# Layer 0 of a decoder trunk: the blocked part of the input projection narrowed to DeltaNet's columns

## The chip, the cores and the metric

The kernel runs on one core of one Trainium2 chip. The metric is the device time of one execution in microseconds; the figure quoted for a kernel is the median of its runs. The profile is a separate, single execution taken by the hardware profiler, and its times are read as shares and durations of that execution.

The engines are named as the profile names them: PE multiplies matrices (PEld is its loading of the stationary operand), DVE works on vectors, ACT evaluates functions and scaled copies, POOL only clears a few tiles here, and SP issues every DMA of this kernel. Each engine takes its instructions in the order in which the planner put them.

## The reference

Two layers, a sequence of 256 tokens, width 2048. In each layer a token mixer and a SwiGLU feed-forward part (FFN) follow one another, each behind an RMS norm that is shifted and scaled by a vector computed from the conditioning vector `c`:

```python
mod = c_act @ w_mod[l] + b_mod[l]                       # [2048] @ [2048, 12288]
shift1, scale1, gate1, shift2, scale2, gate2 = split(mod, 6)
h = rms_norm(x, norm1_gain[l]) * (1 + scale1) + shift1
x = x + gate1 * mixer(h)                                # w_in: 2048 -> 4888, w_out: 2048 -> 2048
h = rms_norm(x, norm2_gain[l]) * (1 + scale2) + shift2
x = x + gate2 * ffn(h)                                  # 2048 -> 2 x 5632 -> 2048
```

The mixer cuts the 4888 columns of `h @ w_in` among three parts. Gated linear attention (GLA) takes 1552 (q and k 512, v 512, gate 512, low rank 16). Sliding-window attention takes 1280 (queries 1024, keys and values 256). Gated DeltaNet takes 2056 (q 512, k 512, v 512, gate with two small vectors 520). Their outputs, 512, 1024 and 512 wide, go side by side through `w_out`. All is float32, and all of `w_mod` (201 MB for both layers), `w_in`, `w_out` and the FFN's weights are read once from HBM.

## The kernel before

**Tiles.** The 256 tokens are two blocks of 128. Activations are the stationary operand, [128 channels, 128 tokens], and weights move past them 512 columns at a time. A step of a product is one chunk of 128 rows of K and up to 1024 columns; it is called a job here (`stream`, L291 to L373). `load` (L311) issues the job's DMA into a [128, 1024] tile and `products` (L340) issues its matmuls for both blocks of tokens. After each job `tick` is called with the job's width over 1024.

**Two ways to multiply.** A split job needs ACT to round the weight (`wh`, L328) and DVE to form the exact rest (`wl`, L329); three fast products then replace one float32 product. A whole job takes the float32 weights as they are, with no work on ACT and DVE, and costs PE four passes in place of three. `WHOLE_IN`, `WHOLE_A` and `WHOLE_OUT` (L43 to L46) say which jobs are whole: in layer 0 all jobs of the blocks below, three chunks of the first GLA product and all of `w_out`; in layer 1 none of these. The weight tiles come from tags `raw`, `wh` and `wl`, three buffers each; whole jobs use the three tags in turn (L316).

**The modulation.** It is a vector times a matrix, done on DVE: `mod_segment` (L199) returns steps; each loads 128 rows of `w_mod` and adds them, times one number a partition, into an accumulator (L218, L221). `finish` (L226) later sums the accumulator over partitions, by four transposes on PE and a reduction on DVE for a shift or a scale (L246 to L254), by two matmuls for a gate (L236). The first shift and first scale of layer 0 are "early": for each block of K, one segment of 512 columns for the shift and one of 512 for the scale, their steps in turn, one DMA of 256 KB and one DVE instruction of 512 columns each; their tiles come from DeltaNet's pool. All later segments have steps of 1024 columns, 512 KB, in two buffers `mraw` and two accumulators `acc`. 96 such steps are due before layer 0's FFN: 32 for gate1, 64 for shift2 and scale2.

**Pacing.** Steps of the modulation stand in one queue, `mods`. `tick` (L271) takes `rate` steps off it for each 1024 columns of other products, and `need` (L282) takes as many as are missing when a value is needed. A step whose kind is in `closed` is not taken by `tick` until it is opened; gate1, shift2 and scale2 of layer 0 are opened as the last block of K begins (L1051). The program order that results is a priority, not the order of execution: a planner goes through the instructions before the run, puts each on its engine when it believes the operands and a free buffer to be there, and prefers what stands earlier in the program. Buffers of one tag are given out in program order.

**Layer 0 before its FFN.** K is cut into four blocks of four chunks (`K_BLOCKS`, L37), each run as soon as its shift and scale are known (loop L1048). For each block: the norm of its channels (`norm`, L436), then the products of four groups of columns (L1026): `qk` (1024), `z` (520), `v` with the keys and values of the sliding window (768), and, at the end of the block, `bq`, the queries of the sliding window (1024). After each block the sums in PSUM are added to tiles in SBUF (`land`, L966 to L975). In the last block `swa_keys` and `gdn` (L538) stand ahead of `bq`. `gdn` is a long chain of small steps: convolution (transposes at L548), decay, the inverse of a triangular matrix by doubling (L683 to L702), two blocks of state. Then comes `swa` (L881), twelve units one behind the other in one PSUM bank `ga` (scores at L897, output at L924), and the products of GLA: A1 (1024 columns, L1080) and A2 (528, L1082), from the last chunk of K to the first. `gla` (L749) uses the bank `ga` as well. `w_out` follows in two sweeps (L1112): 24 jobs over the K of the window and DeltaNet, at two steps of the modulation a job, then 8 jobs over GLA's K, at none. The second norm and the FFN come after them.

**Layer 1** runs the same code with one block of K of all sixteen chunks and all jobs split: `qk`, `z`, `v`, then `gdn`, `bq`, `swa`, A1, A2.

## Time and profile before

| | |
|---|---|
| median of 3 runs | 2591.97 us (2586.66 to 2603.76) |
| profiled execution, span | 2596.9 us, first to last instruction |
| share of the span, PE / DVE / ACT | 94% / 67% / 41% |
| DMA | 600.8 MB, 231 GB/s over the span |
| mean granted PE clock | 0.986 |

The profiled execution has no time of its own besides its span; the span lies 4.9 us (0.2%) above the median of the runs and inside their spread, so what lies around the span is too little to be seen, and differences found in the trace are taken off the median as they are.

The profile's page gives totals; views of the trace give, for chosen stretches, the busy time of each engine, the granted clock and the rate of the DMA (the "stretches" view), the chain of waits, the groups of instructions by source line, or the instructions in order of time. All stretches here count from the first instruction. A busy PE is not a PE at its peak: its matmuls are pipelined, and the view counts the time in which at least one is under way. A float32 matmul shows as two instructions, so eight instructions of 512 columns are the four products of one whole job of 1024 columns.

### The profile page before, as it was taken

The numbers are of one execution on the slowest core, as the hardware profiler recorded it, in microseconds if no ns is written. First come the engines' busy times: TensorE is split into PE (matmuls) and PEld (weight loads), VectorE is DVE, ScalarE is ACT, GpSimd is POOL, SyncE is SP. The second block draws the span as 40 slices with busy tenths as digits, with TensorE's granted clock in tenths as the row PEclk, the third lists the DMA queues.
The fourth block names the chain that finished last, engine by engine and source line by source line (L and its number), as shares of the span: only waits on it lengthen the run. The fifth ranks groups of instructions, "written<-read, shape, count | busy, mean of one in ns | idle before, by whom it ended". The sixth has DMA issues, their size and how long they took to land.

```text
span 2596.9 us, 31018 instructions
## 1 busy us (share of the span) xinstructions
PE 2450.9 (94%) x11164; PEld 1900.8 (73%) x11164; DVE 1752.5 (67%) x2527; ACT 1068.2 (41%) x1582; POOL 26.3 (1%) x72
## 2 busy tenths in 40 slices
PE   3999999979999999999998999999899999999997
PEld 2555785547788777788877788877678878888876
DVE  6767876776666777657678788678674575544555
ACT  2203444124444333444345454654544434344443
POOL 0000000000000000000000000000000000000000
PEclk9999999989999999999999999999999999999999
DMA  9996548767778888868687865356576686666654
GB/s 329 373 317 210 179 133 271 263 214 264 262 261 266 288 281 277 288 194 305 219 274 244 280 209 157 94 176 208 204 258 192 199 281 194 188 193 189 186 179 154
DMA packets 190034, 600.79 MB, mean 231 GB/s; under 512 B 21628, under 2 KB 26268, under 8 KB 189496
## 3 DMA queue, kind: packets, MB, share of 16 engines
q1 hardware_dynamic: 189880, 598.81, 70.6%
q8 instruction: 87, 1.43, 0.2%
q14 instruction: 67, 0.55, 0.1%
HBM read 596.63 MB, written 2.10 MB: 231 GB/s over the span
## 4 chain that ended last, share of the span: by engine, by line
PE 57%; DMA 21%; DVE 12%; issue 6%; ACT 3%; SPq 0%; POOL 0%; DVEq 0%; ACTq 0%; POOLq 0%
PE acc L356 49%; DMA mraw<-in_w_mod 13%; DVE wl L329 4%; DVE acc L221 3%; DMA raw<-in_w_down 3%; DMA raw<-in_w_up 2%; DMA raw<-in_w_gate 1%; DMA raw<-in_w_in 1%; PE ga L830 1%; ACT wh L328 1%; PE mm L401 1%; PE ga L401 1%; PE ga L897 1%; DVE g L221 1%; PE mm L688 1%
## 5 line engine op out<-in xcount | busy, mean ns | idle before, releaser
L356 PE MATMUL acc<-wh,hm 128*128 128x512 f32 (+3 forms) x4872 | 1346.7, 390 | 23.3 <-ACT acc L425 5.3
L328 ACT ACTIVATE wh<-raw 128x1024 fp32r<-128x1024 f32 (+3 forms) x669 | 684.7, 1026 | 993.1 <-PE acc L356 592.1
L329 DVE TENSOR_TENSOR wl<-raw,wh 128x1024 fp32r<-128x1024 f32 (+3 forms) x669 | 785.1, 1179 | 451.0 <-ACT wh L328 449.6
L356 PEld LDWEIGHTS acc<-wh,hm 128*128 128x128 f32 x4872 | 896.1, 190 | 216.6 <-issue 17.0
L356 PE MATMUL acc<-wl,hm 128*128 128x512 f32 (+3 forms) x2484 | 795.2, 394 | 9.9 <-DVE wl L329 7.4
L221 DVE SCALAR_TENSOR_TENSOR acc<-mraw,c_act,acc 128x1024 f32<-128x1024 f32 x320 | 410.3, 1282 | 214.5 <-DMA mraw<-in_w_mod 212.5
L356 PEld LDWEIGHTS acc<-wl,hm 128*128 128x128 f32 x2484 | 458.5, 190 | 116.7 <-DVE wl L329 16.7
L356 PE MATMUL acc<-wh,ahl 128*128 128x512 f32 x560 | 157.9, 396 | 0.0
L356 PEld LDWEIGHTS acc<-wh,ahl 128*128 128x128 f32 x560 | 105.6, 189 | 24.5
L221 DVE SCALAR_TENSOR_TENSOR g<-g,c_act,g 128x512 f32<-128x512 f32 x128 | 88.8, 745 | 13.4 <-DMA g<-in_w_mod 13.4
L356 PE MATMUL acc<-wl,ahl 128*128 128x512 f32 x280 | 90.8, 398 | 4.6 <-DVE wl L329 4.4
L356 PE MATMUL acc<-wh,b 128*128 128x512 f32 (+2 forms) x184 | 75.0, 547 | 3.2 <-ACT b L456 2.1
L356 PE MATMUL acc<-raw,b 128*128 128x512 f32 (+2 forms) x176 | 66.8, 518 | 0.8 <-DVE g L973 0.7
L356 PE MATMUL acc<-wl,b 128*128 128x512 f32 (+2 forms) x176 | 66.1, 513 | 1.3 <-DVE g L973 1.3
L356 PEld LDWEIGHTS acc<-wl,ahl 128*128 128x128 f32 x280 | 52.5, 189 | 19.2 <-DVE wl L329 7.2
L356 PEld LDWEIGHTS acc<-wh,b 128*128 128x128 f32 x184 | 35.3, 198 | 33.3 <-issue 23.9
L456 ACT ACTIVATE b<-mm,mod,mod 128x128 f32<-128x128 f32 x24 | 9.2, 462 | 111.5 <-DVE mod L254 94.0
L356 PEld LDWEIGHTS acc<-wl,b 128*128 128x128 f32 x176 | 32.6, 190 | 28.6 <-issue 21.3
L356 PEld LDWEIGHTS acc<-raw,b 128*128 128x128 f32 x176 | 32.6, 190 | 27.4 <-issue 22.0
L933 DVE TENSOR_TENSOR acc<-acc,gate 128x512 f32<-128x512 f32 x64 | 43.2, 693 | 9.0 <-PE acc L356 8.9
L935 DVE TENSOR_TENSOR xs<-xs,acc 128x512 f32<-128x512 f32 x64 | 42.2, 678 | 0.1
L356 PE MATMUL acc<-raw,hm 128*128 128x512 f32 x88 | 41.8, 597 | 0.0
(320 smaller groups left out, 1662.7 us busy)
## 6 DMA issues: line engine op xcount, KB each, us to landing
mraw<-in_w_mod SPq DMA_DIRECT2D x320, 512.0 KB
raw<-in_w_down SPq DMA_DIRECT2D x176, 512.0 KB
raw<-in_w_gate SPq DMA_DIRECT2D x160, 512.0 KB
raw<-in_w_up SPq DMA_DIRECT2D x160, 512.0 KB
raw<-in_w_in SPq DMA_DIRECT2D x72, 512.0 KB
g<-in_w_mod SPq DMA_DIRECT2D x128, 256.0 KB
raw<-in_w_out SPq DMA_DIRECT2D x43, 512.0 KB
raw<-in_w_in SPq DMA_DIRECT2D x32, 264.0 KB
```

The lines of the kernel that those rows point to most:

```text
L221: V.scalar_tensor_tensor(acc, raw[:, a], c_act[:, i + a:i + a + 1], acc, ALU.mult, ALU.add)
L328: A.activation(wh[:, :width], raw[:, :width], AF.Copy)
L329: V.tensor_tensor(wl[:, :width], raw[:, :width], wh[:, :width].bitcast(F32), ALU.subtract)
L356: TE.matmul(ps[blk, j][:, :segs[j][2]], xa, parts[j][part], start=i == 0 and n == 0, stop=last and n == len(terms) - 1)
L401: TE.transpose(ps[:, j * P:(j + 1) * P], src[:, j * P:(j + 1) * P], ident)
L456: A.activation(h32[:, i], ps[:, i * P:(i + 1) * P], AF.Identity, scale=mod_col[l, 3 * sub + 1, at + i], bias=mod_col[l, 3 * sub, at + i])
L688: TE.matmul(ps[:, s], LT[blk][:, s], Tm[blk][:, s], start=True, stop=True)
L830: TE.matmul(p4[:, g, blk], lhs_t[rows, g, s], rhs_t[rows, g, s], start=True, stop=True)
L897: TE.matmul(ps[:, j * nk:(j + 1) * nk], qT[rows, i + j], kT[rows, g, :nk], start=True, stop=True)
L933: V.tensor_tensor(ps, ps, need(gate_row, (l, part, j)), ALU.mult)
L935: V.tensor_tensor(x_j, x_j, ps, ALU.add)
```

## The change

Only layer 0 before its FFN is changed, and the order of chunks in A1 and A2 of layer 1.

1. **Blocks.** `K_BLOCKS` becomes (2, 4, 4, 4, 2). Only DeltaNet's columns (`qk`, `z`, `v`: 2056) run through them, still whole. The other 2832 columns follow once, in full sweeps of K, split: `bq` (1024) after `gdn`, then one group of the keys and values with half of A2 (256 + 264), `swa_keys`, `swa`, A1 (1024, now all split) and the other half of A2 (264).
2. **First shift and scale side by side.** `first_segment` puts both into one accumulator of 2 x 512 columns. A step of a block of four chunks is two pieces of 512 columns in one DMA and one DVE instruction of 1024; in the two short blocks a step covers two chunks of rows with a DMA and an instruction of 2 x 256 columns for each. One `finish` does both. The weights alternate over three `wl` and two `mraw` buffers, and the whole jobs use `raw` and `wh` alone.
3. **Rates.** 5.0 steps a 1024 columns in the first block, 2.4 in the others; then 1.2 for `bq`, the next group and GLA's products (before: 3.3, in the last block 1.6, in A 1.0). Gate1, shift2 and scale2 are opened only after the last block.
4. **Start.** The two halves of `x` are loaded behind two and four steps of the modulation; constants and gains after them; rotary tables, small parameters and masks at the end of the first block.
5. **Layer 1:** A1 and A2 take the chunks of K in rising order.

```diff
-K_BLOCKS = (4, 4, 4, 4)
+K_BLOCKS = (2, 4, 4, 4, 2)
+RATE_BLOCK = (5.0, 2.4, 2.4, 2.4, 2.4)
-WHOLE_IN = (True, False)
-WHOLE_A = (3, 0)
-RATE_LAST = 1.6
-RATE_IN = (3.3, 0.8)
-RATE_A = (1.0, 1.6)
+RATE_IN = (1.2, 0.8)
+RATE_A = (1.2, 1.6)
...
+    def first_segment(k0, nk):
+        width = nk * P
+        rows = 512 // width
+        st = {}
+        def mods_at(w):
+            return w[:, :2 * D].rearrange("p (s n) -> p s n", s=2)[:, :, k0 * P:k0 * P + width]
+        def step(i):
+            if i == 0:
+                st["acc"] = tl(accp, [P, 1024], "acc")[:, :2 * width]
+                G.memset(st["acc"], 0.0)
+                SY.dma_start(st["acc"][0:1].rearrange("p (s n) -> p s n", s=2),
+                             mods_at(b_mod[0:1]))
+            acc = st["acc"]
+            n = min(rows, KD - i)
+            pool, tag = ((wsp, "wl"), (modp, "mraw"))[which[2] % 5 % 2]
+            which[2] += 1
+            raw = tl(pool, [P, 1024], tag)[:, :n * 2 * width].rearrange("p (a n) -> p a n", a=n)
+            for a in range(n):
+                SY.dma_start(raw[:, a].rearrange("p (s n) -> p s n", s=2),
+                             mods_at(w_mod[0, (i + a) * P:(i + a + 1) * P]))
+            for a in range(n):
+                V.scalar_tensor_tensor(acc, raw[:, a], c_act[:, i + a:i + a + 1], acc,
+                                       ALU.mult, ALU.add)
+            if i + n == KD:
+                fins.append([FIN_LAG, lambda: finish(acc)])
+        def finish(acc):
+            t = tl(smp, [P, 2 * nk], f"modfirst{k0}")
+            for j in range(0, 2 * nk, 4):
+                ps = tl(psf, [P, 512], "fin")
+                for i in range(4):
+                    TE.transpose(ps[:, i * P:(i + 1) * P],
+                                 acc[:, (j + i) * P:(j + i + 1) * P], ident)
+                V.tensor_reduce(t[:, j:j + 4], ps.rearrange("p (a b) -> p a b", a=4),
+                                AX.X, ALU.add)
+            V.scalar_tensor_tensor(t[:, nk:], t[:, nk:], 1.0, gains[:, 0, k0:k0 + nk],
+                                   ALU.add, ALU.mult)
...
+        return [((0, SHIFT1), lambda i=i: step(i)) for i in range(0, KD, rows)]
...
-                pool, tag = ((rawp, "raw"), (wsp, "wh"), (wsp, "wl"))[which[1] % 3]
+                tags = ((rawp, "raw"), (wsp, "wh"), (wsp, "wl"))
+                pool, tag = tags[which[1] % (2 if modulating else 3)]
...
-        for pair in zip(*(mod_segment(0, part, k0, n) for part in (SHIFT1, SCALE1))):
-            mods.extend(pair)
+        mods.extend(first_segment(k0, n))
...
+    for blk in range(NB):
+        for _ in range(2):
+            mods.popleft()[1]()
+        SY.dma_start(xs[:, blk], x[blk * P:(blk + 1) * P])
+    SY.dma_start(ct, consts[:, :N_FULL])
+    SY.dma_start(gains, small[:, :, :2 * KD].rearrange("l p n -> p l n"))
...
-                  "v": ([(wi, CV, 512), (wi, BK, 256)], at_v_kv),
+                  "v": ([(wi, CV, 512), (wi, BK, 256)][:2 if l else 1], at_v_kv),
...
-            rate[1] = RATE_LAST if last and l == 0 else RATE_IN[l]
-            if last:
-                closed.difference_update({(l, GATE1), (l, SHIFT2), (l, SCALE2)})
+            rate[1] = RATE_IN[l] if l else RATE_BLOCK[bi]
...
             if l == 0 and first:
+                load_small(l)
+                rotary()
...
-                kT = swa_keys(pb, both("kv"))
-                gdn(l, pg, [dict(enumerate(both(n))) for n in "qkv"], both("z"), both("cbca"))
-            project("bq")
+        closed.difference_update({(l, GATE1), (l, SHIFT2), (l, SCALE2)})
+        rate[1] = RATE_IN[l]
...
+        if l:
+            kT = swa_keys(pb, both("kv"))
+        gdn(l, pg, [dict(enumerate(both(n))) for n in "qkv"], both("z"), both("cbca"))
+        gemm(groups["bq"][0], range(KD), lhs, land(True, True, at_bq))
+        if l == 0:
+            gemm([(wi, BK, 256), (wi, AG, 264)], range(KD), lhs, land(True, True, at_kv_a2))
+            kT = swa_keys(pb, both("kv"))
         for g in range(2):
             for blk in range(NB):
                 swa(l, pb, blk, g, tiles[f"bq{g}", blk], kT, both("kv"))
         bs.close()
         rate[1] = RATE_A[l]
-        ks = list(range(KD))[::-1]
-        gemm([(wi, AQ, 512), (wi, AV, 512)], ks, lhs, land(True, True, at_a1),
-             whole=ks[:WHOLE_A[l]])
-        gemm([(wi, AG, 264), (wi, AG + 264, 264)], ks, lhs, land(True, True, at_a2))
+        gemm([(wi, AQ, 512), (wi, AV, 512)], range(KD), lhs, land(True, True, at_a1))
+        if l == 0:
+            gemm([(wi, AG + 264, 264)], range(KD), lhs,
+                 land(True, True, lambda blk, j: at_a2(blk, 1)))
+        else:
+            gemm([(wi, AG, 264), (wi, AG + 264, 264)], range(KD), lhs, land(True, True, at_a2))
```

83 lines of the change are left out of this document (42 added, 41 removed).

## The prediction

> **What bounds the kernel now.** I read the page first, then the stretches of layer 0 up to its FFN, then the chain of waits inside them, and at last layer 1's stretch with the same work.
>
> ```profile
> span 2596.9 us, 31018 instructions
> PE 2450.9 (94%) x11164; PEld 1900.8 (73%) x11164; DVE 1752.5 (67%) x2527; ACT 1068.2 (41%) x1582; POOL 26.3 (1%) x72
> ```
>
> The totals say that PE is nearly always under way, but the change touches only the time ahead of layer 0's FFN. The first of the next rows are layer 0, the last two the part of layer 1 from DeltaNet's first transposes on: busy time and (instructions) of PE, PEld, DVE, ACT and POOL, granted clock, DMA share, GB/s.
>
> ```profile
> core 0: us, PE busy (x) PEld busy (x) DVE busy (x) ACT busy (x) POOL busy (x), PEclk, DMA share, GB/s
> 0.00:42.00 42.00, 3.35 (x12) 2.15 (x12) 29.08 (x77) 11.31 (x26) 4.59 (x24) 1.00 0.92 313
> 42.00:160.00 118.00, 116.69 (x357) 64.67 (x358) 87.15 (x143) 20.34 (x48) 2.50 (x16) 1.00 1.01 369
> 160.00:224.00 64.00, 60.89 (x181) 32.52 (x179) 40.46 (x102) 9.00 (x20) 0.00 (x0) 1.00 0.82 276
> 224.00:421.00 197.00, 188.88 (x1088) 146.27 (x1087) 154.36 (x361) 95.41 (x217) 2.86 (x3) 0.97 0.55 173
> 421.00:534.00 113.00, 105.62 (x384) 54.41 (x382) 78.00 (x130) 21.76 (x45) 1.90 (x2) 1.00 0.81 270
> 534.00:576.00 42.00, 33.75 (x85) 16.04 (x86) 36.26 (x65) 11.61 (x28) 0.95 (x1) 0.88 0.71 228
> 1494.00:1692.00 198.00, 197.89 (x1213) 168.12 (x1212) 153.69 (x345) 107.74 (x226) 1.90 (x2) 0.98 0.52 155
> 1692.00:1828.00 136.00, 124.27 (x610) 96.75 (x608) 113.46 (x201) 71.10 (x123) 0.96 (x1) 0.99 0.60 190
> ```
>
> From 42 to 160 us PE (116.69 of 118) and the DMA (share 1.01, 369 GB/s) are full together. Later in layer 0 nothing is: from 224 to 421 DVE is at 78%, the DMA at 55%. There chains set the pace, and their marks are these (first and last start by source line):
>
> ```profile
> L548 PE MATMUL mm<-consts,g x24: 272/273/318, 225.1 to 244.9; 128*128 128x128 f32 x24
> L897 PE MATMUL ga<-kT,b x64: 272/374/792, 258.4 to 413.5; 64*128 64x128 f32 x32, 64*128 64x256 f32 x32
> L971 ACT ACTIVATE hm<-acc x8: 372/492/611, 364.2 to 411.0; 128x512 f32<-128x512 f32 x4, 128x264 f32<-128x264 f32 x2, 128x248 f32<-128x248 f32 x2
> L524 DVE SCALAR_TENSOR_TENSOR a<-ga,grs,hm x8: 340/343/351, 500.2 to 512.0; 128x128 f32<-128x128 f32 x8
> L548 PE MATMUL mm<-consts,g x24: 270/272/276, 1495.0 to 1516.0; 128*128 128x128 f32 x24
> L897 PE MATMUL ga<-kT,b x64: 272/374/480, 1556.0 to 1690.5; 64*128 64x128 f32 x32, 64*128 64x256 f32 x32
> ```
>
> In layer 0 DeltaNet begins at 225, the window's twelve units run from 258 to 414, A ends at 411, and GLA, which uses the window's bank, ends its norm at 512. The modulation's steps by stretch (DVE, busy and count; stretches from 160 on):
>
> ```profile
> 160.00:224.00 64.00, 21.81 (x17) 1.00 0.82 276
> 224.00:421.00 197.00, 45.99 (x36) 0.97 0.55 173
> 421.00:534.00 113.00, 41.07 (x33) 1.00 0.81 270
> 534.00:576.00 42.00, 14.09 (x11) 0.88 0.71 228
> 1494.00:1692.00 198.00, 24.29 (x19) 0.98 0.52 155
> ```
>
> All 96 steps due before the FFN (and one more) lie in the first four rows. The chain (start, us, what) shows them setting the pace in `w_out`, where two buffers of 512 KB take turns between DMA and DVE:
>
> ```profile
> 424.34 4.28 DMA mraw<-in_w_mod
> 428.71 1.30 DVE acc L221
> 430.02 4.01 DMA mraw<-in_w_mod
> ...
> 563.20 1.28 DVE acc L221
> ```
>
> The last one ends at 564.5, and the FFN's first product starts at 575.5 (its row is below), 11 us later. GLA with `w_out`'s eight last jobs (8 x 3.44 = 28 us, price below) would have allowed 512 + 28 + 11 = 551. So the modulation ends layer 0's first half, GLA's chain some 25 us ahead of it, and PE fills the space between.
>
> **The change part by part.**
>
> *Start.* Rows of the chain and of the groups:
>
> ```profile
> 36.48 0.75 DVE g L221
> 42.38 2.07 PE acc L356 x2
> 84.37 3.44 PE acc L356 x8
> L221 DVE SCALAR_TENSOR_TENSOR g<-g,c_act,g 128x512 f32<-128x512 f32 x128 | 88.8, 745 | 13.4 <-DMA g<-in_w_mod 13.4
> L221 DVE SCALAR_TENSOR_TENSOR acc<-mraw,c_act,acc 128x1024 f32<-128x1024 f32 x21 | 26.9, 1282 | 15.9 <-DMA mraw<-in_w_mod 15.9
> ```
>
> The first product waits for 32 steps of 256 KB (8.4 MB) and `x` (2.1 MB); the last step ends at 37.2, two finishes and the norm take 5.1 more. After the change it waits for 4.2 MB of `w_mod`, 2.1 MB of `x` and 0.2 MB of constants, 6.5 MB. At the first stretch's 313 GB/s that is 21 us, and with the same 5.1 us behind it 26: 16 us earlier. DVE needs 16 x 0.745 = 12 us of that, so it no longer sets it. Over all blocks DVE's part falls from 128 x 0.745 = 95 us to 32 x 0.745 + 48 x 1.282 = 85, beside a full DMA: worth nothing.
>
> *Blocks.* A whole job of 1024 columns costs 3.44 us. A chunk of K had 3336 columns, 11.2 us; now 2056, 6.91 us, 111 us for sixteen. But the first shift and scale (33.6 MB) must now pass beside that shorter work. Block 4's modulation is due by the rates before block 2 ends: 5.0 x 4.0 + 2.4 x 8.0 = 39 of the 56 later steps come in blocks 0 and 1, 17 in block 2. So until block 2's last weights the DMA carries 6.5 + 56 x 0.524 + 10 chunks x 1.053 + 1.2 (masks and small tables) = 47.6 MB: 21 + 41.1/0.369 = 132 us. PE could be there at 26 + 69 = 95, so it waits for the DMA, 37 us. Then six chunks remain with no modulation, 41 us of PE, and some 4 us for the last sums: DeltaNet begins at 177, not 225, a gain of 48. From below: PE alone gives 26 + 111 + 4 = 141, which the order of the DMAs excludes unless the last weights are fetched very early; 165 is my end. From above: in the half blocks a row of `w_mod` is 1 KB long instead of 2 KB; the lowest rate of a fortieth in the answer below is 277 GB/s, and at that 8.4 MB cost 7.6 us more; with a poor order of the queue, 190.
>
> ```profile
> GB/s 281 314 351 359 352 372 406 409 283 329 394 346 345 375 386 408 379 345 404 349 393 407 371 391 392 353 277 288 388 406 391 390 353 406 398 377 401 400 312 293
> ```
>
> *From DeltaNet's start to the end of A.* Split jobs, one block of tokens (the six products of a job of 1024 columns take from 594.20 to 595.56), below the FFN's first product:
>
> ```profile
> 575.54 1.22 PE L356 MATMUL acc<-wh,hm 128*128 128x512 f32 x2
> 594.20 0.62 PE L356 MATMUL acc<-wl,hm 128*128 128x512 f32 x2
> 594.65 1.07 PE L356 MATMUL acc<-wh,hm 128*128 128x512 f32 x4
> 595.56 0.62 PE L356 MATMUL acc<-wl,hm 128*128 128x512 f32 x2
> ```
>
> A split job is 2 x 1.36 = 2.72 us, 0.72 less than a whole one: on `bq` 16 x 0.72 = 11.5, on keys and values a quarter of that, 2.9, on A1's three chunks 2.2, together 17 us of PE gone. But this stage gets longer, since `bq` and the keys no longer run before it. Layer 1 is its model: 198 us from DeltaNet's first transposes to the end of A with `bq`, A1 and A2 split, PE at 197.89. Layer 0 adds the 256 columns of keys and values, 16 x 0.68 = 11 us: 209. DVE had 153.69 us there with 19 steps; at 1.2 steps a 1024 columns, 44 job widths give 53 steps, 34 x 1.28 = 44 us more, and the new splits some 6: 204 of 209 us. Two engines at 98% do not mesh without loss, so I take 215, between 205 and 235: A ends at 392. The window's chain agrees: its first score comes 61 us after DeltaNet's start in layer 1, 27 later here for the group with the keys (520 columns, 22 us of PE, among DeltaNet's), at 265, and its units took 135 and 155 us: a last score at 400 to 420, where it was 414; I take 405.
>
> *`w_out` to the FFN.* 53 steps were done at 421 (17 + 36), so at the later pace of 113/33 = 3.42 us some 50 when A ended at 411, and 46 remained: 411 + 46 x 3.42 + 11 = 579, which is nearly the 575.5 seen. Now 53 are done at 392 and 43 remain: 392 + 147 + 11 = 550. GLA's chain, 98 us from the last score to its norm, gives 405 + 98 + 28 + 11 = 542. I take 552, a little behind the later of the two, between 537 and 575.
>
> The sum: 575.5 - 552 = 23 us earlier, made of +48 (blocks), -29 (the stage behind them, 215 for 186) and +4 (160 for 164). From there on the kernel is the same, and PE-bound, so all of it reaches the end. The rising order in layer 1's A is free: the norm has made all chunks long before. The span would be 2574, the median 2592 - 23 = **2569 us**.
>
> **The rivals.**
>
> *The modulation's steps run ahead: 2554.* From 132 to 177 us SP and DVE have room, and a step of gate1 needs only a buffer and an accumulator. The planner does take things early, and SP fills its free time:
>
> ```profile
> 16.32 0.20 ACT L563 ACTIVATE neg_a<-small 128x4 f32<-128x4 f32 x1
> 162.56 0.34 SPq L218 DMA_DIRECT2D mraw<-in_w_mod  x1
> ```
>
> An exponential that belongs to DeltaNet ran at 16 us. With one step each 2.9 us (two in 5.7, by the chain) 15 steps are done before DeltaNet begins, 28 remain at 392, and GLA's chain becomes the last: 400 + 98 + 28 + 11 = 537, a gain of 38. Against it: before, no step of gate1 was issued until 162. Chance 0.25.
>
> *DVE cannot take it: 2592.* DVE was 78% busy in both layers' stages (154.36 of 197, 153.69 of 198), waiting in order for chains. If it reaches 85%, 204 us need 240, A ends at 417, and the rest follows as before: no change. Chance 0.22.
>
> *The modulation falls behind: 2614.* Before, 17 steps were done when DeltaNet began; now gate1 opens only there. If beside DeltaNet steps come as before, 36 in 197 us, SP waiting in order behind weight tiles, then 39 are done at 392 and 57 remain: 392 + 195 + 11 = 598, 22 us late. It decides when fewer than about 46 steps are done at the end of A. For it: SP's waits for those two buffers, the longest in that half.
>
> ```profile
> SPq L218 <- DVE acc L221: 64.5, 38, 6.8
> ```
>
> Against it: program order ties steps to jobs, and before, the 45 due by the rates when A ended (1.6 x 13.0 + 1.0 x 24.3) were there. Chance 0.08.
>
> *A halved PE clock: 2600.* Until 132 us PE waits between jobs, 37 us in all. The granted clock was 1.00 in the stretches where PE was full and 0.88 in the one from 534 to 576, where it idled most. If it halved throughout, ten chunks would take 138 us, not 69, and the blocks would end 31 us later. The Trainium skill, TensorE: Matmul & The Clock Gate, Part 1: The HAM clock gate, says that PE runs at half rate after an idle window of about 3.4 us. By that rule the clock holds here: the DMA brings a job's weights every 3 us or so, and no gap is a window long. The first row, a clock of 1.00 with 3.35 us of PE in 42, does not show the rule at all. Chance 0.04.
>
> The forecast has the remaining 0.41, and its own range is 2552 to 2588. Taking in the second and third case and the bounds above, the range is 2540 to 2604. About 1% (26 us) is what a measurement of this kernel can tell from no change. Faster by more: most of the first rival and the lower part of my own, 0.40. Slower by more: the upper part of the third rival and something for what I do not see, 0.08. Within: 0.52.
>
> **What would show it.** Right: first product near 26 us; DMA share at 0.95 or more up to 130 and falling after; PE's idle time before 132 near 37 us; DeltaNet's first transposes at 165 to 190; 50 to 56 steps done when A ends; DVE above 90% in that stage; the FFN at 540 to 570. Wrong: a step of gate1 before 150 (first rival); A after 410 with DVE at 85% (second); fewer than 46 steps at the end of A, and a chain of DMA and DVE alternating up to the second norm (third); a clock of 0.8 before 130 (fourth). If DeltaNet begins after 200, the count of bytes failed.

## The result, and the profile after

The changed kernel takes 2625.62 us (median of 4 runs, 2617.45 to 2629.83) against 2593.95 for the kernel before on the same chip (2586.66 to 2603.76): a ratio of 1.0117, with an interval of 1.0086 to 1.0149. It is 32 us slower, where 23 us less was forecast.

The first two lines of the page, after the change:

```profile
span 2627.2 us, 31252 instructions
PE 2459.2 (94%) x11272; PEld 1918.3 (73%) x11272; DVE 1775.0 (68%) x2521; ACT 1098.5 (42%) x1628; POOL 26.0 (1%) x65
```

TensorE is busy 8 us longer than before (2450.9), and the span is 30 us longer. The chain of waits of this profile reaches back only to 1692 us, so layer 0 has to be read from stretches and marks. First and last start of the lines that carry layer 0's first half, after (L600 DeltaNet's first transposes, L1024 the evacuations of the late queries `b`, keys `kv` and A `hm`, L925 the doubling of the keys, L927 their transposes, L949 the window's scores, L900 GLA's last products):

```profile
L600 PE MATMUL mm<-consts,g x24: 271/273/447, 181.8 to 201.4; 128*128 128x128 f32 x24
L1024 ACT ACTIVATE b<-acc x4: 597/598/598, 261.8 to 266.3; 128x512 f32<-128x512 f32 x4
L1024 ACT ACTIVATE kv<-acc x2: 364/370/375, 314.4 to 317.8; 128x256 f32<-128x256 f32 x2
L925 DVE COPY kdup<-kv x2: 286/290/293, 320.5 to 332.9; 128x256 f32<-128x256 f32 x2
L927 PE MATMUL mm<-consts,kdup x4: 273/273/328, 332.4 to 333.4; 128*128 128x128 f32 x4
L949 PE MATMUL ga<-kT,b x64: 272/374/481, 334.8 to 460.5; 64*128 64x128 f32 x32, 64*128 64x256 f32 x32
L1024 ACT ACTIVATE hm<-acc x8: 377/488/600, 316.0 to 408.5; 128x512 f32<-128x512 f32 x4, 128x264 f32<-128x264 f32 x2, 128x248 f32<-128x248 f32 x2
L900 PE MATMUL ga<-hm,a x16: 273/275/275, 541.6 to 552.7; 128*128 128x128 f32 x16
```

DeltaNet starts 43 us earlier than before (182 for 225). A ends where it did (409 for 411). The window's scores, 258 to 414 before, now run from 335 to 461, and GLA, in the same PSUM bank behind them, ends 48 us later.

The same half in stretches, with busy time (and instructions) of PE, PEld, DVE, ACT and POOL, granted clock, DMA share and GB/s. The first fence is the kernel before, the second the changed one; they are cut at the first product, DeltaNet's start and 40 us behind it, the end of A, 480 us, the last of `w_out`, and the FFN's first Silu:

```profile
0.00:42.00 42.00, 3.35 (x12) 2.15 (x12) 29.08 (x77) 11.31 (x26) 4.59 (x24) 1.00 0.92 313
42.00:225.00 183.00, 178.14 (x538) 97.36 (x539) 128.61 (x256) 29.34 (x68) 2.50 (x16) 1.00 0.95 337
225.00:265.00 40.00, 39.30 (x149) 22.37 (x149) 32.02 (x102) 23.18 (x47) 0.96 (x1) 0.93 0.39 127
265.00:411.00 146.00, 139.57 (x910) 119.17 (x910) 114.40 (x238) 68.74 (x163) 1.67 (x2) 0.97 0.56 175
411.00:480.00 69.00, 65.65 (x248) 34.40 (x248) 50.04 (x76) 20.17 (x35) 0.23 (x1) 1.00 0.82 281
480.00:567.00 87.00, 77.24 (x232) 36.56 (x230) 63.37 (x104) 13.09 (x38) 1.90 (x2) 1.00 0.80 259
567.00:628.00 61.00, 54.14 (x221) 41.70 (x222) 41.70 (x62) 30.92 (x57) 1.67 (x2) 0.87 0.58 201
```

```profile
0.00:29.00 29.00, 2.36 (x9) 1.55 (x10) 16.45 (x43) 10.25 (x23) 3.01 (x17) 1.00 0.91 317
29.00:182.00 153.00, 129.49 (x380) 68.96 (x380) 122.43 (x187) 30.68 (x72) 3.78 (x16) 0.94 0.94 338
182.00:222.00 40.00, 30.84 (x145) 24.70 (x144) 33.27 (x119) 24.43 (x44) 0.00 (x0) 0.79 0.50 158
222.00:409.00 187.00, 176.19 (x1091) 149.24 (x1089) 150.67 (x286) 85.45 (x172) 2.87 (x3) 0.99 0.71 217
409.00:480.00 71.00, 61.12 (x209) 31.29 (x210) 44.70 (x78) 17.11 (x52) 0.95 (x1) 0.90 0.76 250
480.00:589.00 109.00, 106.71 (x379) 54.80 (x377) 75.26 (x142) 27.76 (x60) 1.90 (x2) 1.00 0.62 202
589.00:650.00 61.00, 51.64 (x211) 39.86 (x210) 40.52 (x53) 30.90 (x57) 0.72 (x1) 0.89 0.57 197
```

An account of TensorE can be made from these rows. A stretch less its busy time is idle; busy time times (1 less the clock) is about what the slower clock took. Until A's end that gives 51 us idle (38.7 + 4.9 + 0.7 + 6.4, of it only 4.9 in the blocks) and 7 by the clock before the change, and 70 (26.6 + 23.5 + 9.2 + 10.8) and 16 after it. So when A ended, at the same time, TensorE had lost 28 us more. By the first Silu it is 71 + 14 against 92 + 28: 35 us more lost, 13 less to do (650 - 120 = 530 us of work, 628 - 85 = 543), and 22 us later. This is bookkeeping: it says where the time was lost, not what would give it back. It is also rough. Taken in stretches of 8 us, the changed kernel and the runs below with the same work in layer 0 (2, 3, 5 and 14 to 18) come out between 528 and 537, and two programs with the same layer 0, the changed kernel and run 18, reach the first Silu at 651.1 and 643.5. So a difference of less than some 8 us between the marks of two profiles says little.

Of the profile's 30 us, 22 are there at the first Silu of layer 0 and 17 at layer 1's DeltaNet (1512 for 1495); the others come in layer 1.

### The profile page after: what moved, and what is told of

It is laid out like the page before. It is cut to its first block, busy times and chain, and to the rows that moved or that the text cites. A ratio compares the mean times of both kernels' runs of the same rounds, so it can differ in the third digit from the quotient of the medians.

```text
span 2627.2 us, 31252 instructions
## 1 busy us (share of the span) xinstructions
PE 2459.2 (94%) x11272; PEld 1918.3 (73%) x11272; DVE 1775.0 (68%) x2521; ACT 1098.5 (42%) x1628; POOL 26.0 (1%) x65
## 5 line engine op out<-in xcount | busy, mean ns | idle before, releaser
L402 PE MATMUL acc<-wh,hm 128*128 128x512 f32 (+3 forms) x5096 | 1414.5, 390 | 31.0 <-ACT wh L374 8.7
L374 ACT ACTIVATE wh<-raw 128x1024 fp32r<-128x1024 f32 (+4 forms) x704 | 711.2, 1013 | 1042.3 <-PE acc L402 626.2
L375 DVE TENSOR_TENSOR wl<-raw,wh 128x1024 fp32r<-128x1024 f32 (+4 forms) x704 | 815.1, 1163 | 434.4 <-ACT wh L374 430.4
L402 PEld LDWEIGHTS acc<-wh,hm 128*128 128x128 f32 x5096 | 936.8, 190 | 232.4 <-issue 26.8
L402 PE MATMUL acc<-wl,hm 128*128 128x512 f32 (+3 forms) x2592 | 832.0, 394 | 17.2 <-DVE wl L375 14.9
L402 PE MATMUL acc<-wh,b 128*128 128x512 f32 (+1 forms) x160 | 65.0, 545 | 9.5 <-DMA wh<-in_w_in 8.5
L402 PE MATMUL acc<-raw,b 128*128 128x512 f32 (+1 forms) x160 | 61.5, 524 | 0.2 <-DMA raw<-in_w_in 0.2
L402 PEld LDWEIGHTS acc<-wh,b 128*128 128x128 f32 x160 | 31.2, 204 | 37.8 <-issue 26.6
L222 DVE SCALAR_TENSOR_TENSOR acc<-wl,c_act,acc 128x1024 f32<-128x1024 f32 (+1 forms) x47 | 50.7, 1079 | 11.8 <-DMA wl<-in_w_mod 5.9
L882 PEld LDWEIGHTS ga<-a 64*128 64x128 f32 x224 | 29.6, 203 | 18.9 <-issue 8.3
L882 PE MATMUL ga<-a 64*128 64x128 f32 x224 | 35.2, 301 | 2.2 <-DVE a L866 1.7
```

The source lines that it names most:

```text
L222: V.scalar_tensor_tensor(acc, raw[:, a], c_act[:, i + a:i + a + 1], acc, ALU.mult, ALU.add)
L374: A.activation(wh[:, :width], raw[:, :width], AF.Copy)
L375: V.tensor_tensor(wl[:, :width], raw[:, :width], wh[:, :width].bitcast(F32), ALU.subtract)
L402: TE.matmul(ps[blk, j][:, :segs[j][2]], xa, parts[j][part], start=i == 0 and n == 0, stop=last and n == len(terms) - 1)
L882: TE.matmul(p4[:, g, blk], lhs_t[rows, g, s], rhs_t[rows, g, s], start=True, stop=True)
```

## The experiments

Marks are in us of the profiled execution: the start of DeltaNet's first transposes, the window's first and last score, GLA's last product, and layer 0's first Silu. The ratio is to the kernel before, measured beside it on the same chip; the times in us come from several chips, so kernels are compared by their ratios.

| run | us | ratio, interval | DeltaNet | scores | GLA | Silu |
|---|---|---|---|---|---|---|
| before | 2593.95 | 1 | 225 | 258-414 | 505 | 629 |
| changed | 2625.62 | 1.0117, 1.0086 to 1.0149 | 182 | 335-461 | 553 | 651 |
| 1 keys in the blocks | 2630.20 | 1.0128, 1.0100 to 1.0157 | 203 | 293-440 | 529 | 658 |
| 2 GLA in other banks | 2608.59 | 1.0050, 1.0030 to 1.0070 | 183 | 333-465 | 485 | 636 |
| 3 keys first | 2647.25 | 1.0207, 1.0180 to 1.0235 | 184 | 345-478 | 567 | 668 |
| 4 all in the blocks | 2667.38 | 1.0281, 1.0242 to 1.0319 | 259 | 269-432 | 528 | 685 |
| 5 no steps beside DeltaNet | 2656.08 | one run | 184 | 324-446 | 531 | 677 |
| 6 blocks of two | 2617.86 | 1.0100, 1.0064 to 1.0137 | 230 | 266-437 | 533 | 652 |
| 7 = 6 and GLA's banks | 2599.42 | 1.0016, 0.9997 to 1.0035 | 228 | 264-431 | 484 | 634 |
| 8 before, GLA's banks | 2580.48 | 0.9951, 0.9928 to 0.9974 | 225 | 258-410 | 470 | 615 |
| 9 six whole jobs | 2641.25 | 1.0180, 1.0143 to 1.0216 | 185 | 337-472 | 561 | 664 |
| 10 = 9 and GLA's banks | 2617.30 | 1.0086, 1.0062 to 1.0110 | 181 | 333-482 | 493 | 645 |
| 11 = 7 and whole jobs | 2585.59 | 0.9982, 0.9961 to 1.0003 | 223 | 232-418 | 462 | 611 |
| 12 = 1 and more steps | 2639.29 | 1.0166, 1.0151 to 1.0181 | 201 | 291-444 | 535 | 659 |
| 13 = 12 and GLA's banks | 2614.31 | 1.0064, 1.0046 to 1.0081 | 203 | 293-451 | 498 | 643 |
| 14 blocks of four | 2637.62 | 1.0139, 1.0108 to 1.0170 | 179 | 338-472 | 561 | 659 |
| 15 = 2, window last in `w_out` | 2611.66 | 1.0055, 1.0040 to 1.0070 | 182 | 337-471 | 486 | 642 |
| 16 = 3, keys in the window's bank | 2638.88 | 1.0170, 1.0144 to 1.0195 | 183 | 325-457 | 549 | 647 |
| 17 = 16 and GLA's banks | 2634.05 | 1.0158, 1.0132 to 1.0183 | 181 | 324-462 | 490 | 640 |
| 18 falling order in layer 1 | 2624.69 | 1.0112, 1.0091 to 1.0133 | 181 | 333-454 | 547 | 644 |

### The blocks: runs 14, 4 and 6

Run 14 gives the changed kernel blocks of four:

```diff
-K_BLOCKS = (2, 4, 4, 4, 2)
-RATE_BLOCK = (5.0, 2.4, 2.4, 2.4, 2.4)
+K_BLOCKS = (4,) * 4
+RATE_BLOCK = (2.4,) * 4
```

> The changed kernel with blocks of (4, 4, 4, 4): the first product has to wait for 8.4 MB of the modulation instead of 4.2, so it comes near 42 (29). Theory (with 2056 columns in the blocks the DMA sets their pace, 47.6 MB until 132, whatever starts first): DeltaNet still starts at 180 to 188, and the time is within 6 us of the changed kernel's 2626. Rival (the early first product is worth its 13 us): DeltaNet at 195, 2638.

DeltaNet's first transposes in run 14:

```profile
L600 PE MATMUL mm<-consts,g x24: 271/272/301, 179.1 to 201.4; 128*128 128x128 f32 x24
```

DeltaNet starts at 179 although the first product waits until 43: the earlier first product (29) moves nothing behind the blocks. The DMA sets their pace: in the changed kernel its share is 1.00 from 29 to 140. The time is 6 us (of 2594, by the ratios) above the changed kernel's, inside both intervals, so about as expected, and not less.

Run 4 puts queries and keys back into the blocks (2, 4, 4, 4, 2), run 6 into eight blocks of two:

```diff
# the moves that follow from it (gdn ahead of the queries, A2 whole) are left out
-for name in ("qk", "z", "v"):
+for name in ("qk", "z", "v", "bq")[:3 if l else 4]:     # "v" with the keys again
# run 6 besides:
+K_BLOCKS = (2,) * 8
+RATE_BLOCK = (1.8,) + (1.4,) * 5 + (1.6,) * 2          # gate1 open in the last two
+RATE_A = (1.4, 1.6)
```

> Keys and queries are both back in the blocks, which stay (2, 4, 4, 4, 2) with the first shift and scale side by side: the new start alone. Theory: the blocks now hold 16 x 11.2 = 179 us of PE again, so that PE waits little for the DMA behind the first product at 29: DeltaNet starts at 215 to 222 (225 before the change), the window's first score near 250, its last near 405, the FFN near 565: about 2582, 10 us ahead of the kernel before. If the new start is worth nothing or costs (short rows of the modulation weights, PE's idle time in the blocks), DeltaNet starts at 225 or later: 2592 or more.

> All columns in eight blocks of two chunks, each with the first shift and scale side by side; gate1's steps may begin in the last two blocks. Theory (a block's work must cover the DMA of the next one's modulation): 22.4 us of TensorE by 7.6 MB, 20.6 us at 0.369 MB/us, so TensorE is full behind the first product at 29: under 10 us idle until DeltaNet, granted clock 1.00, DeltaNet at 213 to 222 (225 before the change), GLA's norm near 505, the FFN's first product near 566, the time near 2583. Rival (each border of blocks costs its sums, norm and wait, 5 us, seven times): 30 us idle, DeltaNet at 240 or later, 2610 or more. If the modulation is last again, the FFN starts some 11 us behind its last step, whatever DeltaNet did.

Run 4, then run 6 (stretches as above; the second line of run 6 is the end of its blocks, the third DeltaNet's start):

```profile
29.00:140.00 111.00, 82.38 (x230) 41.72 (x229) 92.13 (x126) 18.88 (x44) 3.93 (x16) 0.95 0.99 365
580.00:640.00 60.00, 22.72 (x77) 13.90 (x75) 38.89 (x65) 13.99 (x33) 1.90 (x2) 0.67 0.63 197
```

```profile
29.00:180.00 151.00, 148.63 (x446) 80.77 (x445) 136.69 (x262) 26.49 (x63) 3.98 (x18) 0.99 0.97 335
180.00:229.00 49.00, 38.03 (x109) 19.86 (x107) 36.18 (x69) 9.73 (x18) 0.95 (x1) 0.96 0.83 269
229.00:280.00 51.00, 36.82 (x122) 25.06 (x123) 39.48 (x152) 23.17 (x49) 0.00 (x0) 0.67 0.34 111
```

Run 4's theory fell, and its other branch came: DeltaNet at 259, where 225 or later was named. A block of two gives 22 us of TensorE, but the next one, of four, needs 8.4 MB of the modulation first: 29 us idle by 140. At its end the modulation is last (TensorE 23 us of 60). In run 6 the theory holds as long as block and modulation match: 149 of 151 us until 180. There gate1's steps begin beside the last blocks, and 11 us go; then 14 us idle and a clock of 0.67 behind DeltaNet's start. DeltaNet came at 230, between theory and rival, and the time, 2618, missed the 2583 of the theory. So a block has to carry TensorE for the time that the DMA needs for the next block's modulation; columns taken out of it beyond that do not make it shorter.

### Why the window is late: runs 5, 3, 16 and 17

Run 5 takes away the modulation's steps tied to the late products:

```diff
-RATE_IN = (1.2, 0.8)
+RATE_IN = (0.0, 0.8)
```

> The changed kernel with no later step of the modulation tied to the queries' and keys' products beside DeltaNet (rate 0 for 1.2); what is left out there comes later, so the time is not the point, only the marks. Theory A (VectorE has no room beside DeltaNet, 124 us of 152 busy, and the 26 steps of 1.28 us are what is too much): the queries are out near 240 (262), the keys near 285 (316), the first score near 300 (335). Theory B (the 66 us of products are filler that TensorE reaches when DeltaNet leaves it room): the queries still come near 260, the keys after 305, the first score after 320. In either case some 25 steps more are left when A ends, the modulation is last, and the FFN starts 30 to 80 us later than in the changed kernel.

The queries came at 264, the keys at 316 to 318, the first score at 324: theory B. VectorE's 26 steps cost the window 11 us and no more (in the changed kernel and runs 2, 14, 15 and 18, with the same sweep and steps, the first score comes from 333 to 338). The modulation was then last: of its steps, counted from 140 us to A's end, 38 were done, where the changed kernel had 56 (rows of both):

```profile
140.00:416.00 276.00, 48.63 (x38) 0.94 0.59 182
```

```profile
140.00:409.00 269.00, 71.77 (x56) 0.96 0.69 214
```

Run 3 changes the order of the late groups; run 16 adds one word to that, run 17 GLA's banks:

```diff
# run 3
-gemm(groups["bq"][0], range(KD), lhs, land(True, True, at_bq))     # layer 1 keeps this line
-gemm([(wi, BK, 256), (wi, AG, 264)], range(KD), lhs, land(True, True, at_kv_a2))
+gemm([(wi, BK, 256), (wi, BQ, 512)], range(KD), lhs, land(
+    True, True, lambda blk, j: at_bq(blk, 0) if j else at_v_kv(blk, 1)))
 kT = swa_keys(pb, both("kv"))
+gemm([(wi, BQ + 512, 512), (wi, AG, 264)], range(KD), lhs, land(
+    True, True, lambda blk, j: at_a2(blk, 0) if j else at_bq(blk, 1)))
# run 16, in swa_keys
-ps = bank()
+ps = bank("ga")
```

> All columns stay where the change put them; only the order within the sweep differs: the keys with the first 512 query columns, then the other 512 with A2's first part. Theory (the window waits for the whole sweep of 1544 columns, of which its first six units need 768): those 768 are 16 x 2.04 = 33 us of PE and not 66; the first score comes near 285, the last near 420, GLA's norm ends near 520, the FFN starts near 570: about 2592. Rival (VectorE): the first group takes as long as the queries did, 80 us, and the second queries come as late as the keys did: first score near 275, but the second half of the units waits and the last score stays near 450: about 2615.

> The order of the third experiment (keys with the first 512 query columns, out at 250), and the keys' transposes take the window's bank and not one of DeltaNet's two. There the keys were doubled at 254 but their transposes ran at 342, next to DeltaNet's last ones, in whose banks they stood in program order. Theory (it is the bank that makes the window late): the transposes run near 256, the first score near 258 (345 there), the last near 415 (478), GLA's last product near 505 (567), the first Silu 100 to 123 us behind it, at 605 to 628: time near 2598, some 49 us faster than the 2647 of that order alone. Rival 1 (it is TensorE's or VectorE's order that held the transposes, not the bank): they stay behind 330, 2640 or more. Rival 2 (the window is early, but TensorE's idle time sets the half's end): the first score near 258 and the time still 2620 or more.

> The same with GLA in DeltaNet's two banks. Theory: with the window's last output near 425, GLA from A's end at 405 and neither waiting for the other, the banks are worth the 13 us that they gave the kernel before: 2585, ahead of the kernel before by 8. Rival (window and GLA now take turns on VectorE and TensorE, as they do with the banks alone in the changed kernel): the window's last score is 20 us later than without, and the time stays within 6 us of it.

The doubling of the keys and their transposes in run 3, then in run 16 (there also the last halves of the queries' rotation, the first transposes of the queries, and the last product of the second late group):

```profile
L925 DVE COPY kdup<-kv x2: 291/294/297, 254.5 to 343.2; 128x256 f32<-128x256 f32 x2
L927 PE MATMUL mm<-consts,kdup x4: 272/273/273, 341.8 to 343.8; 128*128 128x128 f32 x4
```

```profile
L927 PE MATMUL ga<-consts,kdup x4: 271/272/273, 254.2 to 258.4; 128*128 128x128 f32 x4
L915 DVE TENSOR_TENSOR b<-rope,rope x4: 217/218/219, 265.0 to 327.7; 128x64 f32<-128x64 f32 x4
318.01 0.29 PE L402 MATMUL acc<-wh,hm 128*128 128x264 f32 x1
318.13 0.60 PE L447 MATMUL ga<-consts,b 128*128 128x128 f32 x4
```

In run 3 the keys of the first block of tokens were doubled at 254 and transposed at 342, beside DeltaNet's last transposes. `swa_keys` stands behind `gdn` in the changed order and takes one of DeltaNet's two banks, whose turns go by program order. One word moved the transposes 88 us forward. That is shown. In the changed kernel itself this order costs far less, because its keys come late anyway: they are doubled at 320.5 and transposed at 332.4, so at most 12 us are the bank's, and in run 5, where DeltaNet was done sooner, the same step took 3. The bank's 12 and VectorE's 11 are thus one and the same stretch and do not add up. But the first score came only at 325. The first queries were rotated at 265 and their bank was free from 259, and TensorE transposed them at 318, right behind the last product of the late columns: neither data nor bank held them, only TensorE's own order. So the window stands behind everything that the sweep puts ahead of it, and a faster part of the sweep is not enough. The run is 21 us ahead of run 3 at the first Silu, not the 40 to 60 expected; the same edit acts on layer 1 too, where it is 15 us slower than the changed kernel behind that mark, so its total says little. With GLA's banks as well (run 17) the rival's time came: 2634, within 6 us of run 16's, and not the 2585 of the theory.

### What an earlier window is worth: runs 1 and 12

```diff
-"v": ([(wi, CV, 512), (wi, BK, 256)][:2 if l else 1], at_v_kv),
+"v": ([(wi, CV, 512), (wi, BK, 256)], at_v_kv),      # keys ahead of gdn; A2 whole behind the window
# run 12 besides
-RATE_A = (1.2, 1.6)
+RATE_A = (2.0, 1.6)
```

> Theory (the keys are late): after the change the window's first score waits until 335 us for the keys, whose products run as filler behind DeltaNet's, and GLA stands behind the window in the same PSUM bank. With the keys' columns back in the blocks, PE has 16 x 0.86 = 14 us more there, most of it in its 23 us of waiting for the DMA, so DeltaNet starts at about 190 (182 after the change). The 22 us of the keys' group no longer run beside it, and the window waits for the queries alone: first score near 275, last near 415 (460), GLA's norm done at 513 (558), the FFN at 560 (603). Time about 2583. Rival (VectorE has no room): 124 us of 152 beside DeltaNet were busy; then an earlier window gives its gain back in A and the modulation, A still ends near 409 and the FFN starts near 600: 2620 or more.

> The keys' columns in the blocks, as in the first experiment, which ended GLA 24 us sooner (529 for 553) and was not faster; here the modulation goes at 2.0 steps and not 1.2 beside A, some 19 steps more before A ends. Theory (the late window and GLA behind it cost the changed kernel its time, and in the first experiment the modulation, 10 steps behind when A ended, took GLA's place as the last): the modulation is done before 555, the FFN's first Silu comes 97 to 100 us behind GLA's last product, near 628 (650 after the change), and the time is near 2604. Rival (TensorE's idle time and slow clock set the time whatever is last: it was 124 us there and 120 after the change): no gain, 2620 to 2630.

Run 1 moved the window and GLA, less far than expected (first score 293 where 275 was expected, GLA 24 us earlier), and was no faster: the rival's time. By its count 50 steps of the modulation were done when A ended, and the last of the 96 ran at 581, where the changed kernel's ran at 545. Run 12 had 61 when A ended and the last at 539, and was still no faster: its theory fell too, and its rival (TensorE's idle time and slow clock set the time) came. What took the modulation's place, in run 12's TensorE in order of time:

```profile
489.56 1.98 PE L402 MATMUL acc<-raw,hm 128*128 128x512 f32 x4
492.10 1.16 PE L882 MATMUL ga<-a 64*128 64x128 f32 x8 [0.56 <-DVE a L889]
495.17 2.07 PE L882 MATMUL ga<-a 64*128 64x128 f32 x8 [1.92 <-DVE a L889]
...
519.43 2.07 PE L402 MATMUL acc<-wh,hm 128*128 128x512 f32 x2
```

From 492 to 519 TensorE does GLA alone, turn by turn with VectorE, at half the clock (2.07 us for what took 1.16). No product of `w_out` fills it: the last one into its four accumulators ended at 491.5, and the first `add_gated`, which empties them, comes on VectorE only at 509.5 (458.0 in the changed kernel). Then TensorE is full with `w_out` until 580. The chain got earlier and TensorE's remaining work became the last.

### TensorE's idle time behind DeltaNet's start: runs 9 and 10

```diff
-gemm(groups["bq"][0], range(KD), lhs, land(True, True, at_bq))
+gemm(groups["bq"][0], range(KD), lhs, land(True, True, at_bq),
+     whole=() if l else range(6), modulating=l == 0)
```

> The changed kernel, the first six of the late queries' sixteen jobs whole (no ScalarE and VectorE work, 0.72 us more of TensorE each, 4.3 us in all). Theory (in the 40 us behind DeltaNet's first transposes TensorE loses 9 us idle and 7 by its clock, because the late jobs' splits stand behind DeltaNet's convolutions on VectorE): most of the 16 us comes back, so 8 to 12 us faster than the changed kernel: about 2616. Rival (that loss is slack: the window's serial units behind the keys set the time whatever TensorE does there): the window's first score moves by less than 5 us from 335 and the time stays within 5 us of 2626, or 4 us worse for the work added.

> The same with GLA in DeltaNet's banks. Theory: the two gains are in different stretches and add up: 17 for the banks and 8 to 12 for the whole jobs, about 2599, the kernel before within 10 us. Rival: they do not add up (the one bound takes over from the other): 2606 to 2612.

Run 9, the 40 us behind DeltaNet's start, and the time from A's end (the changed kernel's rows from 182 and from 409 are above):

```profile
182.00:222.00 40.00, 40.00 (x154) 24.79 (x152) 33.59 (x124) 22.31 (x41) 0.00 (x0) 0.96 0.63 202
400.00:490.00 90.00, 73.57 (x242) 40.81 (x241) 56.47 (x95) 20.86 (x63) 1.90 (x2) 0.76 0.71 231
```

The gap was closed, 40 of 40 us busy for 31, and the keys came 9 us sooner; the window did not, and the time got longer by 16. What was saved was lost behind A's end, where TensorE is idle 16 of 90 us and has a clock of 0.76, waiting for the window, for GLA and for the modulation's sums. So the rival was right that idle time there is slack while the window's chain is last, but the loss is more than the 4 us it allowed. With GLA's banks too (run 10) the kernel is 9 us slower than with the banks alone (1.0086 for 1.0050): nothing added up.

### GLA's bank: runs 2, 8, 7, 13 and 15

```diff
 # in gla(): every bank("ga"), and its gated(..., tag_ps="ga")
-ps = bank("ga")
+ps = bank("mm")
```

> Only GLA's PSUM bank differs: it takes the two banks that DeltaNet used, which are free from 334 us. Theory (GLA waits for the window's bank): GLA starts when A ends, near 412 and not at 472; its norm is done near 505 to 515 (558), the FFN starts near 560: about 2585. Rival (GLA waits for its own inputs or for VectorE, and the bank is only where the wait shows): GLA's first matmul stays near 470 to 486, and the time stays within 10 us of the changed kernel's 2626.

> The kernel before, with GLA in DeltaNet's two banks and nothing else. Theory (before the change the modulation ended the half, GLA's chain 25 us ahead of it): GLA ends up to 15 us sooner and the time stays within 6 us of 2594. Rival (GLA's chain was last before the change too): 10 to 17 us faster, 2577 to 2584.

> The blocks of two, and GLA in DeltaNet's two banks. Theory: GLA starts when A ends and not behind the window's last unit, some 10 to 20 us sooner than with the blocks of two alone; the modulation or TensorE's own work is then last, so 0 to 12 us better than the blocks of two alone: about 2577. If GLA's bank is worth something only where the window is late, no difference.

> The same with GLA in DeltaNet's banks. Theory: GLA then ends before 500 and the window's last output, near 447, is the last: 28 whole jobs of w_out, 96 us, and 60 us to the first Silu stand behind it: Silu near 605, the time near 2582. Rival: the gain of the banks alone, 17 us, from wherever the run without them stands; or the modulation is last and there is no gain at all.

> The changed kernel with GLA in DeltaNet's banks, and layer 0's first sweep of w_out takes DeltaNet's four chunks first and the window's eight behind them. Theory (with GLA out of the way, w_out's products behind the window's last output at 474 are what is last, 20 of its 24 first jobs among them): four jobs of 3.44 us move ahead of it, 10 to 14 us faster than with the banks alone (2609): 2597. Rival (TensorE or the modulation is full there, and the order of its products is nothing): 2606 to 2611.

GLA's last products in run 2, then in run 8:

```profile
L900 PE MATMUL mm<-hm,a x16: 272/276/276, 467.1 to 485.0; 128*128 128x128 f32 x16
```

```profile
L848 PE MATMUL mm<-hm,a x16: 272/275/275, 457.7 to 469.7; 128*128 128x128 f32 x16
```

GLA no longer waits for the window, and it is the one edit that gained nearly everywhere: by the ratios 17 us on the changed kernel, 22 on the blocks of two, 24 on run 9, 26 on run 12, 3 on run 16 (inside the intervals), and 13 on the kernel before, against the theory that had it within 6. The sizes were missed elsewhere too: 2609 for 2585 in run 2, 22 us for 0 to 12 in run 7, 2614 for 2582 in run 13. Of run 8's 21 us in the profile, 15 are there at the first Silu; layer 1 gains the rest. Run 8 beats both kernels: 0.9951. In run 2 GLA ends 68 us earlier and the half ends 15 earlier, so something else is last at once. Run 15 took DeltaNet's chunks of `w_out` ahead of the window's for it and found nothing (1.0055 for 1.0050), as its rival said.

Runs 2 and 8 also make a pair, the change with GLA freed from the window in both kernels. TensorE until A's end, in run 2 and in run 8:

```profile
0.00:409.00 409.00, 339.76 (x1630) 244.53 (x1631) 323.22 (x637) 155.23 (x320) 9.66 (x36) 0.96 0.80 266
```

```profile
0.00:409.00 409.00, 359.56 (x1617) 241.40 (x1618) 305.13 (x670) 134.19 (x305) 10.16 (x43) 0.99 0.76 260
```

In this pair the change costs 26 us by the ratios (1.0050 less 0.9951, some 8 us either way) and 22 at the first Silu (636 for 615), nearly as much as without the banks (30 and 22). So GLA's wait for the window's bank costs both kernels, and is not the main part of what makes the changed one slower. What both pairs share lies ahead of A's end, by the bookkeeping of the first section: busy time times clock gives 326 us of TensorE's work done by 409 in run 2 and 356 in run 8, some 30 less, and 322 against 351 without the banks.

### The parts together: run 11

```diff
 # run 7 with RATE_BLOCK = (1.8,) + (1.4,) * 5 + (1.2,) * 2, and
-gemm([(wi, AQ, 512), (wi, AV, 512)], range(KD), lhs, land(True, True, at_a1))
+gemm([(wi, AQ, 512), (wi, AV, 512)], range(KD), lhs, land(True, True, at_a1),
+     whole=() if l else range(4))
```

> The blocks of two with all columns and GLA in DeltaNet's banks, now with the first four jobs of A1 whole again and the modulation at 1.2 and not 1.6 steps in the last two blocks. Theory: of the 21 us that TensorE lost in the 40 us behind DeltaNet's first transposes (10 idle, 11 by its clock) some 15 come back, and 3 of the 15 in the blocks; the whole jobs cost 2.9: about 15 us faster than without (2599): 2584, ahead of the kernel before by 10 us. Rival (VectorE itself, not its order, is what holds that stretch): no gain there, 2600.

Run 11, its blocks and the 40 us behind DeltaNet's start:

```profile
29.00:223.00 194.00, 189.74 (x570) 102.18 (x569) 174.51 (x344) 36.58 (x81) 4.94 (x19) 1.00 0.96 333
223.00:263.00 40.00, 36.75 (x149) 24.43 (x148) 34.13 (x132) 26.82 (x47) 0.00 (x0) 0.83 0.53 177
```

The blocks lose 4 us and no clock, the stretch behind DeltaNet's start 9 (3.3 idle, 6 by the clock) instead of 16. It is 9 us faster than run 7 by the ratios (15 expected) and level with the kernel before (0.9982, 0.9961 to 1.0003; 10 us ahead expected), though its DeltaNet starts 41 us later than the changed kernel's. Against run 8, the old blocks with the same banks, it is not ahead: the early, side-by-side start has not been shown to be worth anything even where its blocks are full.

### Layer 1: run 18

```diff
+ks = range(KD)[::-1] if l else range(KD)      # for A1, and for layer 1's A2
```

> The changed kernel with layer 1's A (its last three thousand columns) going down the chunks of K again, as before the change; layer 0 is left as changed. Behind the FFN of layer 0 the changed kernel is 17 us late, behind layer 1's w_out 29: 12 to 16 us come in layer 1, between the window's last score and GLA's last product (86 us before the change, 107 after). Theory (the rising order, which the prediction put at nothing, does it): the layer-0 marks stay, that stretch returns to about 88 us, and the time is 12 to 16 us less, near 2612. Rival (the rising order is free, and layer 1 differs by what the modulation and the turns of the buffers brought over from layer 0): the stretch stays above 98 us and the time within 5 us of the changed kernel's 2626.

The time is the changed kernel's (1.0112 for 1.0117), and the stretch from the window's last score to GLA's last product is 99 us (107 in the changed kernel, 86 before): the rival. The rising order is free. What makes layer 1 slower stays open. A part of what the profiles show may belong to the one execution: in the changed kernel's, GLA of layer 1 met a slow clock that run 18's did not (below).

## Why the prediction was wrong

**Right.** The first product came at 28.9 (26). The blocks were paced by the DMA, full until 140 (132), and DeltaNet started at 182 (177). Run 14, with the same bytes and a first product 14 us later, started it at 179, as a count of bytes would have it. The rising order cost nothing (run 18). Beside DeltaNet and A TensorE was busy 207 of 227 us, A ended at 409, 17 behind the 392 taken and inside its bounds (205 to 235 us for the stage, 227 measured). From the last score GLA's norm took 97 us (98): its last step began at 557.8. The modulation had 56 steps at A's end (53), was done by 547, and was not last. The bound "fewer than about 46 steps" held where it was met: runs 5 and 4, with 38 and 39, had the modulation last.

**In the forecast's own sum** the blocks gave 43 us (48 taken), the stage behind them took 227 us (215) and cost 41 (29), and from A's end to the FFN's first product, at 590.4, it was 181 us (160), a loss of 17 where a gain of 4 was taken: 15 us later and not 23 earlier. Some 7 more are there at the first Silu, and the rest of the 30 comes in layer 1.

**The step that failed**, the first of two, is the window's start: "61 us after DeltaNet's start in layer 1, 27 later here for the group with the keys", at 265. It came at 335, 70 us later, and the last score at 460 instead of 405; everything behind it follows at the forecast's own distances (460 + 97 + 28 = 585, against a last product of `w_out` that ended at 588.8). The model was layer 1, where the keys are made ahead of DeltaNet. Here both late groups are filler beside it: 66 us of products took until 318, 136 us behind DeltaNet's start and not 88. Behind that stood two orders that the prediction did not read in the code: the keys' transposes share DeltaNet's banks in program order (12 us at most here, 88 in run 3), and TensorE's own order has the window behind the late columns (run 16). VectorE, the second rival, had a share of 11 us (run 5), in the same 12; it was 82% busy from 182 to 334. Over the whole stage it was busy 184 of 227 us, 81%: the sign "above 90%" failed, and stage and share lie between the forecast and that rival (85%, A's end at 417).

**The gain of 48** for an early DeltaNet, the second step that failed, was no gain. The work left out of the blocks came back beside DeltaNet, where before the change TensorE was already busy 179 of 186 us, and the blocks shrank by less than the work that left them: 30 us (183 to 153) for 69 of products (sixteen chunks at 6.9 and not 11.2 us). TensorE waited 23 us there by 140 (37 forecast by 132) and lost 8 more to the clock, for which the forecast had no term. With the 16 us lost in the 40 behind DeltaNet's start (3 before), A ended where it had, with the window's second half still to do and some 30 us less of TensorE's work done. Runs 2 and 8 show that this part of the cost stays when GLA no longer waits for the window.

**One bound per stage** was the wrong form. "GLA's chain some 25 us ahead" of the modulation did not mean that GLA was worth nothing: run 8 gained 13 us from it alone. Modulation, GLA's chain and TensorE's own work are tied: steps come with `w_out`'s products, and each filled gap is missing later. Runs 9, 1 and 12 removed one loss each and got nothing; in each another bound stood close behind.

**A reading** in the forecast was off by little: the last of the 96 steps before the change ran from 566.0 to 567.2 and not from 563.2 to 564.5, so the FFN's first product followed it by 8 us and not 11, and the forecast's 550 would have been 547.

**The rivals.** The first came true in its sign, a step of gate1 at 147, with GLA's chain last, but the FFN's first product came at 590 and not at 537. The clock's rival had the mechanism in small: 0.83 in the first 40 us of the blocks and 0.94 over all of them, where it was put at 1.00, some 8 us, not 31.

**Open:** how the 32 us divide between TensorE's lost time and the late window, since every run that mended one changed the other, and runs 9 and 10, which closed one of TensorE's gaps, gained nothing; why run 12 is slower than run 1 in spite of more modulation done; and the part that arises in layer 1.

## What to carry to other kernels

Moving work out of a stage that the DMA paces shortens it by less than the work moved, here by 30 us for 69: TensorE then idles there and has more to do in the next stage. Before moving a producer behind another chain in program order, look at what the consumer shares with that chain, a PSUM bank whose turns go by program order above all, and where it then stands in each engine's order. If two chains that could overlap share a single bank, separate them first: here that paid in the kernel before as well (13 us; nothing else was tried there).

## What the runs showed of the hardware

**The clock follows single gaps.** In the changed kernel's blocks the mean wait between jobs is short, but some are not (TensorE in order of time, then its stretches):

```profile
43.24 3.80 PE L402 MATMUL acc<-wh,b 128*128 128x260 f32 x8 [5.67 <-DMA wh<-in_w_in]
```

```profile
44.00:48.00 4.00, 4.00 (x11) 3.09 (x10) 2.88 (x3) 0.05 (x1) 0.00 (x0) 0.50 1.05 407
64.00:68.00 4.00, 3.02 (x7) 1.70 (x8) 2.61 (x10) 2.73 (x7) 0.00 (x0) 0.50 1.05 409
76.00:80.00 4.00, 4.00 (x11) 1.83 (x10) 1.70 (x3) 0.00 (x0) 0.00 (x0) 1.00 1.05 407
```

Behind an idle 5.67 us, which ended at 43.24, the granted clock was 0.50 from 44 to 48. A gap of 3.56 us ended at 60.92 and one of 3.30 at 64.98, and it was 0.50 again from 64 to 68; at 76, with no gap, it was 1.00. The Trainium skill, TensorE: Matmul & The Clock Gate, Part 1: The HAM clock gate, puts the idle window at about 3.4 us; the gap of 5.67 agrees. The prediction applied the rule to a mean gap and so expected a clock of 1.00.

**A slow clock without a gap.** In layer 1's GLA the changed kernel's profiled execution has TensorE at 0.50 while it is busy all the time:

```profile
1772.00:1776.00 4.00, 3.90 (x12) 2.98 (x13) 3.01 (x5) 0.00 (x0) 0.00 (x0) 0.50 0.00 0
1776.00:1780.00 4.00, 4.00 (x13) 2.93 (x13) 2.42 (x4) 0.00 (x0) 0.00 (x0) 0.50 0.35 106
1784.00:1788.00 4.00, 4.00 (x19) 2.76 (x19) 3.46 (x4) 1.65 (x3) 0.00 (x0) 1.00 0.72 219
```

From 1764 to 1784 no idle time before an instruction is longer than 0.39 us there. Run 18's profile has 1.00 through the same part of GLA. What sets it is not known from these runs.
